# Joined 512-column high pass in channel-major products; output gates, gate logits and branch products with tokens stationary and 512 weight columns moving

## The chip, the cores and the metric

The kernel runs on one core of one Trainium2 chip. The metric is device time in microseconds, smaller is better. The matrix engine (TensorE, PE in the rows) multiplies a stationary block of 128 by 128, loaded into it first, with a moving block of up to 512 columns, and writes sums to PSUM. VectorE (DVE), ScalarE (ACT) and GpSimd (POOL) do the elementwise work; SyncE (SP) issues nearly all weight transfers.

## The reference

One layer of a decoder trunk, 256 tokens, width 2048, all in float32. Cut to what matters here:

```python
proj = jnp.einsum('bsd,de->bse', x, w_in)            # 2048 -> 14 thousand columns
(lru_x, lru_y, gla_q, gla_k, gla_v, gla_alr, gla_r,
 dn_qkv, dn_b, dn_a, dn_z, gate_logits) = jnp.split(proj, ...)
y_lru = _rg_lru_branch(lru_x, lru_y, ...)            # ends in  h * gelu(lru_y)
y_gla = _gla_branch(..., gla_r, ...)                 # ends in  rmsnorm(o) * silu(gla_r)
y_dn  = _gated_deltanet_branch(dn_qkv, ..., dn_z)    # ends in  rmsnorm(o) * silu(dn_z)
gates = jax.nn.sigmoid(gate_logits.reshape(bsz, seq, 3, D_MODEL) + b_gate)
merged = (gates[:, :, 0] * (y_lru @ w_branch[0])
          + gates[:, :, 1] * (y_gla @ w_branch[1])
          + gates[:, :, 2] * (y_dn @ w_branch[2]))
x = _layernorm(ALPHA * x + merged @ w_out, ln1_g, ln1_b)
h = jnp.square(jax.nn.relu(x @ mlp_w1 + mlp_b1)) @ mlp_w2 + mlp_b2
x = _layernorm(ALPHA * x + h, ln2_g, ln2_b)
```

## The kernel before

**Three products for one.** Each float32 operand is split into a high part in the rounded matmul type and a low part, the rest: `split` lets ACT make `hi` (line 94) and DVE make `lo` (line 95). A product is then high weight by high input, high by low, and low by high, three matmuls into one sum.

**Jobs.** All large products are a list of jobs, and `run_jobs` goes through it. A job loads 1 MB of weights (512 KB for a branch product), splits them, multiplies, and evacuates. The loads and splits of the next job stand ahead of the products of this one; `raw`, `hi` and `lo` have three buffers each, and a job uses one `raw` and two of `hi` and `lo`.

**Two layouts.** A channel-major job (`jobB`, `mmB`, lines 121 to 140) holds one 128x128 weight tile stationary, and the 256 tokens move: the sum `accB` has 128 channels by 256 tokens. It has 16 tiles of the contraction, so 48 matmuls of 256 columns; the weight tile `hi` is loaded once for `xh` (124) and once for `xl` (125). A token-major job (GLA's values, `accV`, lines 467 to 469; the output product `accO`; the second MLP product `accM`) holds 128 tokens stationary and moves 512 weight columns: 24 matmuls of 512 columns per job.

**The order of the work.** Four channel tiles together with x itself (`acc0`), then the projections of RG-LRU, GLA and DeltaNet, then for each of the three branches b sixteen pairs of one gate job (`evac_gate`) and one branch job (`job_branch`, `evac_branch`: 24 matmuls), with the eight jobs of DeltaNet's output gate behind b = 0. Then the output product, the norm, the first MLP product (`js`, 64 channel tiles, of which three go with the norm, `accH`), and the second.

**Mixers.** The small steps of the recurrences (`gen_small`, `gen_lru`, `gen_gla`, `gen_dn_*`) are generators that `pump` advances between the jobs, by a budget of DVE and ACT time per job. The Tile framework then orders the instructions of each engine and sets the semaphores; each engine runs its own queue in order.

Of the kernel before, what the change touches and what calls it, by code (L numbers as in the profile page):

```python
# [25 lines left out]
# columns of the packed per-channel parameters  # L26
# [8 lines left out]
C_BG = C_DN_G + 1  # L35
C_B1 = C_BG + 48
# [6 lines left out]
# columns of the packed constants  # L43
# [10 lines left out]
# columns of the parameters that are needed later  # L54
# [4 lines left out]
# rows of the small projections in their channel tile  # L59
# [6 lines left out]
def trunk_kernel(ctx, tc, xw, xtok, par, lat, con, wab, wa2, wB, wV, wBr, wO, w1, w2a, w2b, rows, out):  # L66
# [23 lines left out]
    def t1_tile(name, shape, dt=F32):  # L90
        return sm.tile(shape, dt, tag="t1", name=name, bufs=6)
# [6 lines left out]
    xh = [big.tile([P, 8, T], F32R, tag="xh", name=f"xh{i}", bufs=2) for i in range(2)]  # L98
    xl = [big.tile([P, 8, T], F32R, tag="xl", name=f"xl{i}", bufs=2) for i in range(2)]
# [21 lines left out]
    def mmB(acc, job, rh, rl, part, start, stop):  # L121
# [7 lines left out]
    def jobB(src, evac, rh=None, rl=None):  # L129
        rh, rl = rh or xh, rl or xl  # L130
        job = Job(src, 8 * len(rh), None, None)

        def mm():
            acc = mm_tile("accB")
            n = len(rh)
            for i in range(n):
                mmB(acc[:, :T], job, rh[i], rl[i], i, i == 0, i == n - 1)
            evac(acc[:, :T])
# [24 lines left out]
    # ---- inputs that the first jobs need  # L163
    # x and the first four channel tiles together, one slice of the contraction at a time
# [11 lines left out]
    for k in range(KT):  # L176
# [10 lines left out]
        for i in range(G0):  # L187
            o = acc0[i][:, :T]
            te.matmul(o, lhsT=h[:, i, :], rhs=kh, start=k == 0, stop=False)
            te.matmul(o, lhsT=h[:, i, :], rhs=kl, start=False, stop=False)  # L190
            te.matmul(o, lhsT=l[:, i, :], rhs=kh, start=False, stop=k == KT - 1)
# [25 lines left out]
    def col(c):  # L217
        return pt[:, c:c + 1]
# [9 lines left out]
    bgh = const.tile([P, 48], F32, name="bgh")  # L228
    ve.tensor_scalar(bgh, pt[:, C_BG:C_BG + 48], 0.5, None, ALU.mult)
# [3 lines left out]
    # ---- small projections: GLA's low rank, beta and decay of DeltaNet  # L233
# [9 lines left out]
    def evac_small(acc):  # L243
        ve.tensor_scalar(zs, acc, col(C_DTB), col(C_SGN), ALU.add, ALU.mult)
        live.append(gen_small())

    def gen_small():
        # GLA's log decay: 16 gk per head
# [47 lines left out]
        # beta, g: token rows  # L296
# [19 lines left out]
        # GLA: cumulated log decay in chunks of 64, and its exponentials  # L316
# [15 lines left out]

    yh = {}
# [6 lines left out]
    # ---- LRU  # L340
# [10 lines left out]
    def evac_lru_x(k):  # L351
        def f(acc):
            if k % 4 == 0:
                lru["xc", k // 4] = b4_tile("xc", [P, 4, T])
            conv(acc, lru["xc", k // 4][:, k % 4, :], C_LRU_W + 4 * k, col(C_LRU_B + k))
        return f

    def evac_lru_y(k):
        def f(acc):
            if k % 4 == 0:  # L360
                lru["y", k // 4] = b4_tile("yb", [P, 4, T])
            sc.copy(lru["y", k // 4][:, k % 4, :], acc)
# [4 lines left out]
    def gen_lru(hf):  # L367
# [14 lines left out]
        # gelu  # L382
# [32 lines left out]
    # ---- GLA  # L415
    gla = {}

    def evac_gla_q(h):
        def f(acc):
            if h == 0:  # L420
                gla["qe"] = b4_tile("qe", [P, 4, T])
            ve.scalar_tensor_tensor(gla["qe"][:, h, :], acc, P ** -0.5, gla["eb"][:, h, :], ALU.mult, ALU.mult)
        return f

    def evac_gla_k(h):
        def f(acc):
            if h == 0:
                gla["ke"] = b4_tile("ke", [P, 4, T])
                gla["kd"] = b4_tile("kd", [P, 4, T])
            ve.tensor_tensor(gla["ke"][:, h, :], acc, gla["enb"][:, h, :], ALU.mult)  # L430
# [3 lines left out]
    def silu2(acc, dst, use_act=True):  # L434
        """dst = 2 silu(acc)"""
# [4 lines left out]
    def evac_gla_r(k):  # L440
        def f(acc):
            if k % 4 == 0:
                gla["r", k // 4] = b4_tile("rr", [P, 4, T])
            silu2(acc, gla["r", k // 4][:, k % 4, :])
            if k == 7:
                live.append(gen_gla())
        return f

    def jobs_gla_v():
        gla["v"] = {}  # L450
        accs = {}
        jobs = []
        for nh in range(2):
            for kg in range(4):
                job = Job(wV[nh, kg], 16, None, None)

                def mm(job=job, nh=nh, kg=kg):
                    if kg == 0:
                        accs[nh] = [mm_tile("accV") for _ in range(NT)]
                    for k4 in range(4):  # L460
                        k = 4 * kg + k4
                        hi = job.hi[k4 // 2].rearrange("p k c -> p (k c)")[:, (k4 % 2) * 512:(k4 % 2) * 512 + 512]
                        lo = job.lo[k4 // 2].rearrange("p k c -> p (k c)")[:, (k4 % 2) * 512:(k4 % 2) * 512 + 512]
                        for tt in range(NT):
                            sh = xh[k // 8][:, k % 8, tt * P:(tt + 1) * P]
# [878 lines left out]
```

## Time and profile before

| | |
|---|---|
| median of 3 runs | 1744.58 us (1744.1 to 1745.21) |
| span of the profiled execution, first to last instruction | 1743.0 us |
| PE busy | 1722.7 us (99%), 12782 matmuls |
| DVE, ACT, POOL busy | 61%, 51%, 4% |
| bytes moved | 319.96 MB, mean 184 GB/s |

The time of the profiled execution itself is its span of 1743.0 us and about 1.6 us around it, if it ran as the median run did. A matmul's printed duration runs to the modelled end of its pipeline and overlaps the next one; how fast PE goes is read from the distance between two starts.

### The profile page before, as it was taken

How to read it: one execution, taken by the hardware profiler on the slowest of the kernel's cores; microseconds unless marked ns; L12 is line 12 of the kernel's file. 1: busy time of each engine (PE TensorE's matmuls, PEld its weight loads, DVE VectorE, ACT ScalarE, POOL GpSimd, SP SyncE). 2: the span in 40 equal slices, each digit the busy share in tenths (PEclk: the TensorE clock that was granted, in tenths of full speed). 3: DMA queues.
4: the chain of work that ended last, by engine and by line, in shares of the span. 5: the costliest groups of instructions: out<-in, count | busy, mean ns of one | idle time of the engine just before them, and what ended most of it. 6: DMA issues, size and time to landing. Idle time of an engine off the chain costs nothing.

```text
span 1743.0 us, 30261 instructions
## 1 busy us (share of the span) xinstructions
PE 1722.7 (99%) x12782; PEld 1644.9 (94%) x12782; DVE 1058.2 (61%) x1353; ACT 889.8 (51%) x1209; POOL 76.7 (4%) x112
## 2 busy tenths in 40 slices
PE   8999999999999999999999999999999999999997
PEld 8999898999999999999998899999999988888897
DVE  7876456876765585565555675444444455576767
ACT  6785445785344443444444455554545444455553
POOL 0000000000120203000000000000000000000000
PEclk9999999999999999999999999999999999999999
DMA  8445543444564446355566835555545455555552
GB/s 328 150 170 187 197 173 125 166 170 149 184 194 148 161 170 187 130 181 182 184 217 223 308 109 209 190 177 187 187 177 193 172 192 195 194 193 193 203 193 97
DMA packets 52536, 319.96 MB, mean 184 GB/s; under 512 B 6752, under 2 KB 7136, under 8 KB 18992
## 3 DMA queue, kind: packets, MB, share of 16 engines
q1 hardware_dynamic: 49280, 310.92, 50.3%
q0 software_dynamic: 2976, 6.84, 1.5%
q8 instruction: 100, 1.64, 0.4%
q14 instruction: 36, 0.29, 0.0%
q10 hardware_dynamic: 144, 0.26, 0.0%
HBM read 315.09 MB, written 2.88 MB: 182 GB/s over the span
## 4 chain that ended last, share of the span: by engine, by line
PE 97%; DVE 1%; DMA 1%; ACT 0%; issue 0%; SPq 0%; DVEq 0%
PE accB L124 19%; PE accB L127 19%; PE accB L125 19%; PE accM L1200 7%; PE accM L1201 7%; PE accM L1199 7%; PE accB L982 3%; PE accB L984 3%; PE accB L986 3%; PE accO L917 1%; PE accO L915 1%; PE accO L916 1%; PE accV L467 1%; PE accV L469 1%; PE accV L468 1%; DMA raw<-in_w_dram 0%
## 5 line engine op out<-in xcount | busy, mean ns | idle before, releaser
L95 DVE TENSOR_TENSOR lo<-raw,hi 128x1024 fp32r<-128x1024 f32 (+2 forms) x584 | 708.6, 1216 | 541.6 <-ACT hi L94 537.8
L94 ACT CAST hi<-raw 128x1024 fp32r<-128x1024 f32 (+2 forms) x584 | 602.4, 1034 | 757.1 <-PE accB L125 406.0
L124 PE MATMUL accB<-xh,hi 128*128 128x256 f32 x1744 | 431.0, 285 | 0.0
L125 PE MATMUL accB<-xl,hi 128*128 128x256 f32 x1744 | 427.9, 283 | 0.0
L124 PEld LDWEIGHTS accB<-xh,hi 128*128 128x128 f32 x1744 | 334.4, 192 | 2.4 <-issue 1.4
L125 PEld LDWEIGHTS accB<-xl,hi 128*128 128x128 f32 x1744 | 334.5, 192 | 0.4
L127 PE MATMUL accB<-xh,lo 128*128 128x256 f32 x1744 | 244.9, 283 | 0.0
L124 PE MATMUL accB<-x1h,hi 128*128 128x256 f32 x976 | 239.7, 283 | 0.0
L125 PE MATMUL accB<-x1l,hi 128*128 128x256 f32 x976 | 239.5, 283 | 0.0
L127 PEld LDWEIGHTS accB<-xh,lo 128*128 128x128 f32 x1744 | 225.0, 192 | 0.1
L1200 PE MATMUL accM<-hi,hl 128*128 128x512 f32 (+1 forms) x608 | 212.8, 350 | 0.0
L1199 PE MATMUL accM<-hi,hh 128*128 128x512 f32 (+1 forms) x608 | 212.8, 350 | 0.0
L1201 PE MATMUL accM<-lo,hh 128*128 128x512 f32 (+1 forms) x608 | 212.8, 350 | 0.0
L125 PEld LDWEIGHTS accB<-x1l,hi 128*128 128x128 f32 x976 | 187.4, 192 | 0.0
L124 PEld LDWEIGHTS accB<-x1h,hi 128*128 128x128 f32 x976 | 187.4, 192 | 0.0
L127 PE MATMUL accB<-x1h,lo 128*128 128x256 f32 x976 | 137.0, 283 | 0.0
L1199 PEld LDWEIGHTS accM<-hi,hh 128*128 128x128 f32 x608 | 115.1, 189 | 15.1
L1200 PEld LDWEIGHTS accM<-hi,hl 128*128 128x128 f32 x608 | 115.1, 189 | 15.0
L1201 PEld LDWEIGHTS accM<-lo,hh 128*128 128x128 f32 x608 | 115.1, 189 | 14.8
L127 PEld LDWEIGHTS accB<-x1h,lo 128*128 128x128 f32 x976 | 125.9, 192 | 0.0
L982 PE MATMUL accB<-yh,hi 128*128 128x256 f32 x384 | 109.8, 286 | 0.0
L986 PE MATMUL accB<-yh,lo 128*128 128x256 f32 x384 | 108.7, 283 | 0.0
(308 smaller groups left out, 1861.3 us busy)
## 6 DMA issues: line engine op xcount, KB each, us to landing
raw<-in_wB_dram SPq DMA_DIRECT2D x109, 1024.0 KB, 4.8
raw<-in_w_dram SPq DMA_DIRECT2D x64, 1024.0 KB, 4.8
raw<-in_w2a_dram SPq DMA_DIRECT2D x32, 1024.0 KB, 4.8
raw<-in_w2b_dram SPq DMA_DIRECT2D x32, 1024.0 KB, 4.8
raw<-in_wBr_dram SPq DMA_DIRECT2D x48, 512.0 KB, 3.4
raw<-in_wO_dram SPq DMA_DIRECT2D x16, 1024.0 KB, 4.9
raw<-in_wV_dram SPq DMA_DIRECT2D x8, 1024.0 KB, 4.8
raw<-in_xw_dram SPq DMA_DIRECT2D x15, 384.0 KB, 8.0
```

Source lines behind the costliest of these rows:

```text
L94: i1 = sc.copy(hi, raw)
L95: i2 = ve.tensor_tensor(lo, raw, hi.bitcast(F32), ALU.subtract)
L124: te.matmul(acc, lhsT=hi[:, k, :], rhs=rh[:, k, :], start=start and k == 0, stop=False)
L125: te.matmul(acc, lhsT=hi[:, k, :], rhs=rl[:, k, :], start=False, stop=False)
L127: te.matmul(acc, lhsT=lo[:, k, :], rhs=rh[:, k, :], start=False, stop=stop and k == 7)
L467: te.matmul(accs[nh][tt], lhsT=sh, rhs=hi, start=k == 0, stop=False)
L982: te.matmul(acc[:, :T], lhsT=job.hi[0][:, 4 * i + k, :], rhs=yh[b][i][:, k, :], start=i == 0 and k == 0, stop=False)
L984: te.matmul(acc[:, :T], lhsT=job.hi[0][:, 4 * i + k, :], rhs=yl[b][i][:, k, :], start=False, stop=False)
L986: te.matmul(acc[:, :T], lhsT=job.lo[0][:, 4 * i + k, :], rhs=yh[b][i][:, k, :], start=False, stop=i == 1 and k == 3)
L1199: te.matmul(t, lhsT=sh, rhs=hi, start=k == 0, stop=False)
L1200: te.matmul(t, lhsT=sl, rhs=hi, start=False, stop=False)
L1201: te.matmul(t, lhsT=sh, rhs=lo, start=False, stop=k == NK2 - 1)
```

## The change

Three things are changed, and the mathematics is the same.

Channel-major jobs hold the high and the low part of the input side by side (`pairs`, tiles `xx` of 2 x 256 tokens). One matmul of 512 columns takes the place of the two of 256 with the same weight tile; the left half of the sum is high by high, the right half high by low. The low weights go by the 256 high columns into the left half. `both` adds the halves: ACT copies the right one, DVE adds the left. `evac_h` has this add too, and its square moves from ACT to DVE.

GLA's output gate r, DeltaNet's output gate z, the gate logits and the branch products become token-major jobs (`jobs_tok`), with 4 blocks of 512 columns per 2048. All of them load 1 MB per job now. The gate's bias was a per-channel operand of ACT; it is now a row that POOL's queue loads into one buffer for each block (`load_bg`), and DVE adds it.

The merged sum is then token-major, so it is transposed on PE ahead of the output product (`gen_merged`: 4 blocks x 2 x 4 = 32 transposes of 128x128). Both branch gates are now multiplied in ahead of the transposes that these branches had already, and the split behind them reads PSUM directly (`to_branch_scaled`).

```diff
+    def pairs(name):
+        t = [big.tile([P, 8, 2, T], F32R, tag="xx", name=f"{name}{i}", bufs=2) for i in range(2)]
+        return t, [v[:, :, 0, :] for v in t], [v[:, :, 1, :] for v in t]
...
         for k in range(8):
-            te.matmul(acc, lhsT=hi[:, k, :], rhs=rh[:, k, :], start=start and k == 0, stop=False)
-            te.matmul(acc, lhsT=hi[:, k, :], rhs=rl[:, k, :], start=False, stop=False)
+            te.matmul(acc, lhsT=hi[:, k, :], rhs=flat(r[:, k]), start=start and k == 0, stop=False)
         for k in range(8):
-            te.matmul(acc, lhsT=lo[:, k, :], rhs=rh[:, k, :], start=False, stop=stop and k == 7)
...
+            te.matmul(acc[:, :T], lhsT=lo[:, k, :], rhs=r[:, k, 0, :], start=False, stop=stop and k == 7)
+
+    def both(acc, dst=None):
+        s = dst if dst is not None else t1_tile("sum", [P, T])
+        sc.copy(s, acc[:, T:])
+        ve.tensor_tensor(s, acc[:, :T], s, ALU.add)
+        return s
...
-            conv(acc, c, C_DN_W + 4 * k)
+            conv(both(acc), c, C_DN_W + 4 * k)
...
+    def jobs_tok(src, nkg, rows_of, evac, nm):
+        accs = []
+        jobs = []
+        for kg in range(nkg):
+            job = Job(src[kg], 16, None, None)
+            def mm(job=job, kg=kg):
+                if kg == 0:
+                    accs.extend(mm_tile(nm) for _ in range(NT))
+                for k4 in range(4):
+                    k = 4 * kg + k4
...
+                    rh, rl = rows_of(k)
+                    for tt in range(NT):
+                        sh, sl = rh[:, tt * P:(tt + 1) * P], rl[:, tt * P:(tt + 1) * P]
+                        te.matmul(accs[tt], lhsT=sh, rhs=hi, start=k == 0, stop=False)
+                        te.matmul(accs[tt], lhsT=sl, rhs=hi, start=False, stop=False)
+                        te.matmul(accs[tt], lhsT=sh, rhs=lo, start=False, stop=k == 4 * nkg - 1)
+                if kg == nkg - 1:
+                    for tt in range(NT):
+                        evac(tt, accs[tt])
...
-            sc.activation(t, acc, AF.Tanh, scale=0.5, bias=bgh[:, b * 16 + d:b * 16 + d + 1])
+    def load_bg(b, cb):
+        t = sm.tile([P, 512], F32, tag="bg", name="bgrow", bufs=1)
+        gp.dma_start(t, bg[b:b + 1, cb * 512:(cb + 1) * 512].to_broadcast([P, 512]))
+        gates["row"] = t
...
+            ve.tensor_tensor(t, acc, gates["row"], ALU.add)
+            sc.activation(t, t, AF.Tanh, scale=0.5)
...
-            ve.scalar_tensor_tensor(u, t, 1.0, acc, ALU.add, ALU.mult)
-            gp.tensor_tensor(m, m, u, ALU.add)
...
+            ve.scalar_tensor_tensor(t, t, 1.0, acc, ALU.add, ALU.mult)
+            gp.tensor_tensor(m, m, t, ALU.add)
+            if b == 2 and tt == NT - 1:
+                live.append(gen_merged(cb))
...
+        for kp in range(2):
+            p = mx_tile("p_m")
+            for a in range(2):
+                c = (cb % 2) * 512 + (2 * kp + a) * P
+                for tt in range(NT):
+                    te.transpose(p[:, a * T + tt * P:a * T + (tt + 1) * P], mg[tt, cb // 2][:, c:c + P], ident)
...
     for b in range(3):
-        for d in range(16):
-            jobs.append(jobB(wB[65 + b * 16 + d], evac_gate(b, d)))
-            jobs.append(job_branch(b, d))
+        for cb in range(4):
+            hooks[len(jobs)] = lambda b=b, cb=cb: load_bg(b, cb)
+            jobs += jobs_tok(wG[b, cb], 4, x_rows, evac_gate(b, cb), "accG")
+            if (b, cb) == (2, 0):
+                hooks[len(jobs)] = finish
+            jobs += jobs_tok(wBr[b, cb], 2, y_rows(b), evac_branch(b, cb), "accY")
...
-            sc.activation(t, acc, AF.Relu, bias=col(C_B1 + c))
-            sc.activation(h[c // 4][:, c % 4, :], t, AF.Square)
+            sc.activation(t, acc[:, T:], AF.Identity, bias=col(C_B1 + c))
+            ve.tensor_tensor(t, acc[:, :T], t, ALU.add)
+            ve.scalar_tensor_tensor(h[c // 4][:, c % 4, :], t, 0.0, t, ALU.max, ALU.mult)
```

How the instructions stand now is shown at three places. First PE, at the end of the second channel-major job, where GLA's first small product `p_gk` comes in. Before:

```order
L125 MATMUL accB<-xl_78,hi 128x256
L127 MATMUL accB<-xh_76,lo 128x256 x8
L258 MATMUL p_gk<-zs,wa_sb 128x256 x4
L124 MATMUL accB<-xh_75,hi 128x256
L125 MATMUL accB<-xl_77,hi 128x256
```

In the changed kernel (`xx_75` and `xx_76` are the two halves of the joined input):

```order
L131 MATMUL accB<-xx_76,hi 128x512 x8
L133 MATMUL accB<-xx_76,lo 128x256 x8
L267 MATMUL p_gk<-zs,wa_sb 128x256 x4
L131 MATMUL accB<-xx_75,hi 128x512 x8
L133 MATMUL accB<-xx_75,lo 128x256 x8
```

Sixteen alternating matmuls of 256 columns became eight of 512; the low pass and the place of the mixer's product stayed.

Second DVE, in the first stage, between the two splits `lo` of the third job. Before:

```order
L95 TENSOR_TENSOR lo_534<-raw_531,hi_533 128x1024
L349 SCALAR_TENSOR_TENSOR xc_432<-accB_474,pt_116,xc_432 128x255
L269 COPY lw_608<-lt_409 128x8
L272 SCALAR_TENSOR_TENSOR le_605<-lz_604 128x256
L349 SCALAR_TENSOR_TENSOR xc_432<-accB_474,pt_116,xc_432 128x254
L95 TENSOR_TENSOR lo_538<-raw_531,hi_537 128x1024
```

In the changed kernel:

```order
L94 TENSOR_TENSOR lo_463<-raw_460,hi_462 128x1024
L362 SCALAR_TENSOR_TENSOR xc_367<-sum_382,pt_114,xc_367 128x254
L139 TENSOR_TENSOR sum_449<-accB_416,sum_449 128x256
L362 SCALAR_TENSOR_TENSOR xc_367<-sum_382,pt_114,xc_367 128x253
L94 TENSOR_TENSOR lo_467<-raw_460,hi_466 128x1024
```

The add of the halves (`sum_449`) stands between the splits, and the convolution of the first four tiles (`sum_382`) has slid to here, one job later than before.

Third POOL's queue, around DeltaNet's first triangular inverse (`md` to `dDT` are its round trips through memory). Before:

```order
L694 MEMSET X 32x1024
L695 MEMSET X 32x32
L710 DMA xd<-X 8x32x32 x4
L710 DMA xtd<-mb 8x32x32 x4
L715 MEMSET dD 128x1024
L715 MEMSET dDT 128x1024
L718 DMA dD<-xd 32x8x32 x4
L718 DMA dDT<-xtd 32x8x32 x4
```

In the changed kernel (`bgrow` is the one buffer of the gate's bias):

```order
L710 MEMSET X 32x1024
L881 DMA bgrow<-in_bg_dram 128x512
L711 MEMSET X 32x32
L731 MEMSET dD 128x1024
L731 MEMSET dDT 128x1024
L881 DMA bgrow<-in_bg_dram 128x512
L726 DMA xd<-X 8x32x32 x4
L726 DMA xtd<-mb 8x32x32 x4
L734 DMA dD<-xd 32x8x32 x4
L734 DMA dDT<-xtd 32x8x32 x4
L881 DMA bgrow<-in_bg_dram 128x512 x2
```

Each load of the row waits until DVE has read the row before, and stands in one queue with the inverse's transfers, ahead of some and behind others.

## Rows read from the trace of the kernel before

**Rows 1.** Page: span, and busy time of each engine.

```profile
span 1743.0 us, 30261 instructions
PE 1722.7 (99%) x12782; PEld 1644.9 (94%) x12782; DVE 1058.2 (61%) x1353; ACT 889.8 (51%) x1209; POOL 76.7 (4%) x112
```

**Rows 2.** Page: chain that ended last, shares of the span by engine.

```profile
PE 97%; DVE 1%; DMA 1%; ACT 0%; issue 0%; SPq 0%; DVEq 0%
```

**Rows 3.** Waits of PE, all of them: for whom, total us, times, longest.

```profile
PE acc L189 <- ACT hi L94: 4.2, 2, 3.8
PE p_x L1077 <- DVE xt L1069: 2.0, 1, 2.0
PE accO L917 <- DVE lo L95: 1.3, 1, 1.3
PE acc L191 <- DVE lo L95: 0.2, 1, 0.2
```

**Rows 4.** Timeline of PE in a channel-major job: start, duration, instruction.

```profile
301.53 0.28 PE L124 MATMUL accB<-xh,hi 128*128 128x256 f32 x1
...
302.97 0.28 PE L124 MATMUL accB<-xh,hi 128*128 128x256 f32 x1
```

**Rows 5.** Timeline of PE in a token-major job.

```profile
179.69 0.39 PE L468 MATMUL accV<-hi,xl 128*128 128x512 f32 x1
...
185.81 0.39 PE L468 MATMUL accV<-hi,xl 128*128 128x512 f32 x1
```

**Rows 6.** Timeline of PE around four transposes.

```profile
744.65 0.28 PE L986 MATMUL accB<-yh,lo 128*128 128x256 f32 x1
744.77 0.60 PE L848 MATMUL p_dot<-ct,do 128*128 128x128 f32 x4
...
745.32 0.28 PE L125 MATMUL accB<-xl,hi 128*128 128x256 f32 x1
```

**Rows 7.** Windows by stage: length, busy us (instructions) by engine, clock, DMA share, GB/s.

```profile
29.80:160.40 130.60, 130.60 (x1056) 129.10 (x1055) 100.48 (x133) 96.31 (x130) 0.00 (x0) 1.00 0.49 177
...
249.80:403.70 153.90, 153.90 (x1231) 145.93 (x1230) 118.16 (x195) 102.45 (x163) 0.00 (x0) 1.00 0.44 154
403.70:910.60 506.90, 506.90 (x4231) 503.98 (x4231) 307.14 (x440) 216.61 (x296) 67.01 (x91) 1.00 0.52 173
...
1025.90:1377.00 351.10, 351.10 (x2929) 351.10 (x2928) 163.79 (x137) 179.84 (x252) 1.62 (x3) 1.00 0.52 185
```

**Rows 8.** Groups of DVE by shape: count | busy, mean ns | idle before.

```profile
L95 DVE TENSOR_TENSOR lo<-raw,hi 128x1024 fp32r<-128x1024 f32 x565 | 696.3, 1234 | 539.0 <-ACT hi L94 535.6 <-ACT th L437 1.9 <-PE accB L127 0.8
...
L349 DVE SCALAR_TENSOR_TENSOR cv<-accB,pt,cv 128x254 f32<-128x254 f32 x24 | 11.5, 479 | 0.4
...
L878 DVE SCALAR_TENSOR_TENSOR mg<-gate,accB 128x256 f32<-128x256 f32 x16 | 6.6, 415 | 17.2 <-PE accB L986 17.2
...
L1170 DVE TENSOR_TENSOR xt<-accM,xt 128x512 f32<-128x512 f32 x6 | 4.0, 684 | 0.7 <-PE accM L1201 0.7
```

**Rows 9.** Groups of ACT by shape.

```profile
L1038 ACT ACTIVATE h<-hr 128x256 f32<-128x256 f32 x64 | 26.7, 418 | 1.9
...
L362 ACT COPY yb<-accB 128x256 f32<-128x256 f32 x8 | 2.9, 364 | 0.0
```

**Rows 10.** Windows of 25 us, columns as in rows 7.

```profile
25.00:50.00 25.00, 25.00 (x201) 24.35 (x200) 22.14 (x44) 16.87 (x26) 0.00 (x0) 1.00 0.66 247
...
325.00:350.00 25.00, 25.00 (x207) 24.80 (x206) 22.46 (x37) 18.58 (x30) 0.00 (x0) 1.00 0.49 171
```

**Rows 11.** Timelines of DVE and PE: one split, and the pass that reads it.

```profile
58.24 1.22 DVE L95 TENSOR_TENSOR lo<-raw,hi 128x1024 fp32r<-128x1024 f32 x1
...
62.83 1.12 PE L127 MATMUL accB<-xh,lo 128*128 128x256 f32 x8
```

**Rows 12.** Groups of POOL by shape.

```profile
L882 POOL TENSOR_TENSOR mg<-mg,gb 128x256 f32<-128x256 f32 x32 | 26.0, 813 | 262.1 <-DVE gb L881 262.1
```

**Rows 13.** DMA issues: count, KB each, median us to landing.

```profile
r_g<-in_rows_dram POOLq DMA_DIRECT2D x4, 512.0 KB, 7.0
```

More of the change, by code (lines that the diff above doesn't have):

```diff
@@ L90, in t1_tile @@
     def t1_tile(name, shape, dt=F32):
-        return sm.tile(shape, dt, tag="t1", name=name, bufs=6)
+        return sm.tile(shape, dt, tag="t1", name=name, bufs=7)
     def split(raw, hi, lo):
@@ L96, in split @@
         return i1, i2
-    xh = [big.tile([P, 8, T], F32R, tag="xh", name=f"xh{i}", bufs=2) for i in range(2)]
-    xl = [big.tile([P, 8, T], F32R, tag="xl", name=f"xl{i}", bufs=2) for i in range(2)]
+    def pairs(name):
+        t = [big.tile([P, 8, 2, T], F32R, tag="xx", name=f"{name}{i}", bufs=2) for i in range(2)]
+        return t, [v[:, :, 0, :] for v in t], [v[:, :, 1, :] for v in t]
+    xx, xh, xl = pairs("xx")
     class Job:
@@ L361, in f @@
                 lru["y", k // 4] = b4_tile("yb", [P, 4, T])
-            sc.copy(lru["y", k // 4][:, k % 4, :], acc)
+            both(acc, lru["y", k // 4][:, k % 4, :])
             if k % 4 == 3:
@@ new lines, in x_rows, with evac_gla_v, f, evac_silu @@
+    def x_rows(k):
+        return xh[k // 8][:, k % 8, :], xl[k // 8][:, k % 8, :]
+    def evac_gla_v(nh):
+        def f(tt, acc):
+            if nh == 0:
+                gla["v", tt] = b4_tile(f"v{tt}", [P, 4, 256])
+            (sc.copy if tt else ve.tensor_copy)(
+                gla["v", tt].rearrange("p h c -> p (h c)")[:, nh * 512:(nh + 1) * 512], acc)
+        return f
+    def evac_silu(dic, nm, nh, after=None):
+        def f(tt, acc):
+            if nh == 0:
+                dic[nm, tt] = b4_tile(nm, [P, 1024])
+            t = t2_tile("th", [P, 512])
+            sc.activation(t, acc, AF.Tanh, scale=0.5)
+            ve.scalar_tensor_tensor(dic[nm, tt][:, nh * 512:(nh + 1) * 512], t, 1.0, acc, ALU.add, ALU.mult)
+            if nh == 1 and tt == NT - 1 and after:
+                live.append(after())
+        return f
@@ L996, in trunk_kernel @@
         if b == 0:
-            for k in range(8):
-                jobs.append(jobB(wB[57 + k], evac_dn_z(k)))
+            for nh in range(2):
+                jobs += jobs_tok(wZ[nh], 4, x_rows, evac_silu(dn, "dz", nh), "accZ")
     n_mix = len(jobs)
@@ L1017, in before_out @@
     def before_out():
[L1018 removed]
         dummy = sm.tile([P, 1], F32, tag="dummy", name="dummy", bufs=1)
[L1020 removed]
+        sc.activation(dummy, gates["row"][:, 0:1], AF.Sqrt, scale=0.0, bias=eps[:, 3:4])
         for tt in range(NT):
@@ L1025, in before_out @@
                 nc.sync.dma_start(xt[tt, i], xtok[tt * P:(tt + 1) * P, i * 1024:(i + 1) * 1024])
-    x1h = [big.tile([P, 8, T], F32R, tag="xh", name=f"x1h{i}", bufs=2) for i in range(2)]
-    x1l = [big.tile([P, 8, T], F32R, tag="xl", name=f"x1l{i}", bufs=2) for i in range(2)]
+    xx1, x1h, x1l = pairs("xx1")
     h = []
@@ L1268, in lay_out @@
     small[:, R_A:R_A + 8] = da
-    wB = np.concatenate([tiles(t) for t in (small, lx, ly, gq, gk, gr, qkv, dz, gl)], 0)
-    wBr = np.stack([tiles(f["w_branch"][b]) for b in range(3)], 0)
+    wB = np.concatenate([tiles(t) for t in (small, lx, ly, gq, gk, qkv)], 0)
+    wG = np.stack([blocks(gl[:, b * D:(b + 1) * D], 4, 512) for b in range(3)], 0)
+    wBr = np.stack([blocks(f["w_branch"][b], 4, 512) for b in range(3)], 0)
     def ch(v):
```

212 lines of the change are left out of this document (83 added, 129 removed).

## The prediction

> **What bounds the kernel now.** I began with the page. PE is busy for 1722.7 of 1743.0 us [rows 1], and the chain that ended last lies on PE for 97% of the span [rows 2]. A busy PE may still wait inside its pipeline, so the view of PE's waits comes next: the reader is to see that it has four lines, 7.7 us in all, at the start and around the first norm [rows 3]. So for nearly all of the span PE issues without a pause, and what counts is the distance between its starts. It is read in two stretches without mixers. In a channel-major job 12 steps take 302.97 - 301.53 = 1.44 us, 120.0 ns for 256 columns [rows 4]. In a token-major job 27 steps take 185.81 - 179.69 = 6.12 us, 226.7 ns for 512 columns [rows 5]. Two matmuls of 256 cost 240.0 ns and one of 512 costs 226.7: **13.3 ns for each pair that becomes one**. The granted clock is 1.00 in all four stages of rows 7, the upper level of 2.4 GHz, so no change of clock is in this difference.
>
> The windows by stage then say how far the other engines are from taking over: DVE has 100.5 of 130.6 us in the first projections, 118.2 of 153.9 in DeltaNet's, 307.1 of 506.9 in gates and branches, 163.8 of 351.1 in the first MLP product [rows 7]. PE does not wait for it anywhere there [rows 3], but finer windows reach 22.1 and 22.5 of 25 [rows 10].
>
> **The change, part by part.** *Pairs joined.* Channel-major: the first four tiles 4 x 16 = 64 pairs, 45 jobs of 16 that keep this layout 720, the first MLP product 61 x 16 = 976 and its three tiles that go with the norm 48. Token-major: r and z lose 16 x 48 matmuls of 256 and get 16 x 24 of 512, so 384 pairs; the gate logits 48 x 24 = 1152; the branch products 48 x 12 = 576. Together 3920. The 48 beside the norm I count at nothing, since PE waits there for DVE already [rows 3]; if they did count it would be 0.6 us. 3872 x 13.33 ns = **-51.6 us**.
>
> For the branch, gate, r and z products the price is that of a row of the same form: tokens stationary, 512 weight columns moving [rows 5]. For the channel-major join no row shows 512 columns against a stationary weight tile. I take the same 226.7, because both are a 128x128 load and 512 float32 columns; the other bound is 240, where 1808 of the pairs give nothing (24.1 us less).
>
> The Trainium skill's page TensorE: Matmul & The Clock Gate, section Back-to-back issue gap, speaks against a gain of this size: it gives the gap of a lone stream as columns over 2.4 GHz plus about 2.5 ns, so 109 ns for 256 columns and 216 for 512, and a pair that is joined would save only that 2.5 ns. By that, 3872 pairs give 9.7 us. This case's rows have 120.0 and 226.7, so each start costs 13.3 ns beyond its columns here, and they decide.
>
> *Transposes of the merged sum.* 32 more on PE. Four of them moved the matmuls behind by 0.43 us: the second matmul after them starts at 745.32, and at the steady 120 ns it would have been 744.65 + 2 x 0.12 = 744.89 [rows 6]. So 0.108 us each, **+3.5 us**. They wait for POOL's add. Behind the last product of a block DVE needs 0.68 us per token half [rows 8], and POOL two adds of 512 columns, each some 1.6 us as twice its 0.81 for 256 [rows 12] (an estimate): some 4 us. They stand 24 matmuls, 5.4 us, behind that product, so I count no wait; if DVE has two splits of 1.23 us [rows 8] ahead of the evacuation it is about 1 us for each of the four blocks.
>
> *The adds of the halves.* Each of 45 jobs and 4 first tiles gets an ACT copy (0.364 us [rows 9]) and a DVE add (0.42, as the 256-column DVE reading PSUM [rows 8]). An MLP job gets two DVE instructions of 0.42 and loses ACT's square of 0.418 [rows 9]. Nothing of this is on PE; what hides it is PE's own time, and what is late if the cover goes is the split `lo`, for which PE waits. By stage:
> First projections, 21 jobs and the four tiles: DVE 100.5 + 25 x 0.42 = 111.0; PE 130.6 - 21 x 0.213 = 126.1, so 88%. In the hottest window DVE goes from 22.1 to some 25.5 (4 tiles, 4 jobs) against 24.1 us of PE: over by 1.4. The cover is the lead: a split that ends at 58.24 + 1.22 = 59.46 is read at 62.83, 3.4 us later [rows 11]. From 28 us to there DVE gets 9 adds, 3.8 us, and PE comes 1.1 us earlier, so this lead is used up. ACT also carries two table loads more. I take **2 us** of waits, bounds 0 and 5.
> DeltaNet's projections, 24 jobs: 118.2 + 10.1 - 3 (GLA's tail loses eight 0.42 us instructions) = 125 of 148.8, 84%; the hottest window 22.5 + 1.8 = 24.3 of 24.1. **1 us**, bounds 0 and 4.
> Gates and branches: 24 bias adds of 0.68 and smaller items give DVE about 12 us more: 319 of 485, 66%. But the triangular inverses and the chain of small products behind them share DVE with evacuations that are now 0.68 long. **1 us**, bounds 0 and 3.
> First MLP product: DVE 163.8 + 61 x 0.84 = 215 of 338, 64%; ACT falls to 154. Nothing; a job has 2 us of DVE to spare, and without that cover each 0.1 us per job would cost 6.
> Together **+4 us** (0 to 12).
>
> *The bias row.* 12 loads of 256 KB on POOL's queue, one buffer. The row is read a whole block (four jobs, 21.8 us) after it is asked for; 512 KB from the same queue land in 7.0 us [rows 13]. Nothing.
> *Transfers.* Gates and branches needed 1.5 MB in 48 x 120 + 24 x 120 ns = 8.64 us, now 1 MB in 5.44: 193 GB/s on demand, as the first MLP stage draws 185 [rows 7]. Nothing; the weight queue waits for nothing new.
>
> **The sum.** -51.6 + 3.5 + 4 = -44.1 us against the profiled span of 1743.0: 1698.9. The median of the runs is 1.6 us above the span, 1744.58, so **1700.5 us**.
>
> **The rivals.**
> *DVE comes too late.* The waits are 10 to 25 us rather than 4, since order within a queue and not mean load decides. For it: hottest windows over 100%. Against it: before, windows at 90% made PE wait not once [rows 3, 10]. 1706 to 1722 us.
> *The weight-stationary join gives little.* If what a matmul costs beyond its columns stayed with the halves, 1808 pairs would give nothing: 1724.6; if no pair of either layout gave more than about 2.5 ns, 1742.4. Against it: rows 5 have the same columns at 226.7 ns. The second of these is where the page's formula would put it.
> *More than the sum.* No waits, and the 48 pairs count: 1695.9, or a little less with the waits at the norm shortened.
> *Slower, by the bias row.* DVE's add of a block waits for the row, the splits queue behind the add, and PE behind the splits. In POOL's queue the row stands behind the inverse's transfers, or behind the last reader of its one buffer. A row that misses its block by x makes PE wait about x - 3.4 (the lead of rows 11). It is slower only when that adds to more than 48 us, 4 us in each of 12 blocks, so if rows land some 29 us after the asking; 7.0 us speaks against it. From 1748 us.
> *It does nothing:* the 3920 issues were hidden behind something else. PE's unbroken pace speaks against it. 1744.6.
>
> **How the numbers follow.** Forecast (1695.5 to 1706) 0.73; late DVE 0.13; join of little worth 0.05; more than the sum 0.04; slower 0.03; nothing 0.02. The range of eight in ten is the forecast, down to 1694 for the case above it and up to 1712 for the near half of late DVE: about 0.82. A measurement of this kernel tells about 0.2% from no change, 3.5 us; faster has 0.95, same 0.02, slower 0.03.
>
> **What would show each step.** The distance of starts in the eight joined matmuls should be 226.7 ns, and a channel-major job 8 x 2 x (226.7 + 120) = 5.55 us instead of 5.76. From the first gate to the output product it should be about 484 us instead of 506.9, the first MLP product 338 instead of 351.1. PE's waits should name `lo` on DVE before 130 us and around 300 to 400, a few us in all. The transposes should show no wait for POOL over 1 us. I am wrong if the joined distance is near 240, or if waits for DVE pass 12 us; a wait of DVE for the bias row would show the slower rival.

## The result and the profile after

The changed kernel takes 1711.41 us (median of 4 runs, 1710.71 to 1714.08) where the kernel before takes 1744.34: 0.9816 of its time, 95% interval 0.9802 to 0.983. It is clear of no change and faster, as forecast, but by 33 us where 44 were forecast. The profiled execution has a span of 1709.4 us, 33.6 less than before.

The page of the changed kernel, which answers to [rows 1]:

```profile
span 1709.4 us, 22528 instructions
...
PE 1683.4 (98%) x8894; PEld 1443.0 (84%) x8894; DVE 1126.4 (66%) x1511; ACT 877.7 (51%) x1164; POOL 85.8 (5%) x108
```

There are 3888 fewer matmuls, as counted (3920 joined, 32 transposes more). PE's waits, all of them, beside [rows 3]:

```profile
PE acc L201 <- ACT hi L93: 6.8, 2, 4.2
PE p_bg L312 <- DVE lr L308: 2.6, 1, 2.6
PE p_x L1103 <- DVE xt L1095: 1.3, 1, 1.3
PE p_x L1103 <- issue: 1.1, 1, 1.1
PE p_i L753 <- DVE q L746: 1.0, 1, 1.0
PE accB L133 <- DVE lo L94: 0.4, 1, 0.4
PE accB L131 <- ACT hi L93: 0.3, 1, 0.3
```

The first line is at the very start, where before it was 4.2 us in two waits; the waits on `p_bg`, `accB` and `p_i` are new, and that on `accO` is gone. Where the rest went is read from the time between the first matmuls of the stages, in both traces:

| from the first matmul of ... to that of ... | before | after | difference | forecast |
|---|---|---|---|---|
| start of the span to the first job | 29.79 | 33.93 | +4.1 | -0.9 |
| first job to GLA's values | 130.61 | 131.70 | +1.1 | -2.5 |
| GLA's values to the first gate (values, r, DeltaNet) | 250.58 | 243.90 | -6.7 | -6.7 |
| first gate to the output product | 499.66 | 479.09 | -20.6 | -22.0 |
| output product to the transposes of the norm | 90.01 | 90.45 | +0.4 | +0.9 |
| these to the second MLP product | 376.33 | 364.58 | -11.8 | -13.0 |
| second MLP product to the end | 366.02 | 365.75 | -0.3 | 0 |

The last column puts the forecast's terms where they belong: the pairs of each stage at 13.3 ns, 24 transposes in the gates' stage and 8 in the output product's, the waits of 2, 1 and 1 us. (The cut at 403.70 in rows 7 lies 7.3 us early, a good job: before, the first gate job starts at 410.98. That moved these 7.3 us between two stages of the forecast, and left its sum as it was.) Most of the gap of 10.5 us is in the first two lines, before any of the new token-major jobs has run. The windows of the two long stages, columns as in rows 7:

```profile
33.93:165.63 131.70, 128.25 (x720) 111.24 (x719) 107.59 (x158) 104.13 (x148) 0.00 (x0) 1.00 0.48 167
...
409.53:888.62 479.09, 478.11 (x2274) 398.21 (x2273) 312.75 (x435) 211.21 (x272) 72.80 (x85) 1.00 0.55 190
```

In the first projections PE loses 3.4 of 131.7 us while DVE is busy for 82% and ACT for 79%. Mean load names no culprit.

**The distance of the joined matmuls.** Timeline of PE in a gate job and in a job of the first MLP product:

```profile
412.05 0.39 PE L474 MATMUL accG<-lo,xx 128*128 128x512 f32 x1
...
414.77 0.39 PE L474 MATMUL accG<-lo,xx 128*128 128x512 f32 x1
...
1100.63 2.00 PE L131 MATMUL accB<-xx,hi 128*128 128x512 f32 x8
1102.47 1.12 PE L133 MATMUL accB<-xx,lo 128*128 128x256 f32 x8
...
1106.22 2.00 PE L131 MATMUL accB<-xx,hi 128*128 128x512 f32 x8
```

In the gate job 12 steps take 2.72 us, 226.7 ns each, the price that was taken. In the channel-major job eight joined matmuls take 1.84 us, 230 ns each in the mean, and a whole job 1106.22 - 1100.63 = 5.59 us (5.587 over 50 jobs) where 5.547 were forecast. That is 5.76 - 5.587 = 0.173 us for 16 pairs, 10.8 ns a pair and not 13.3. The starts one by one say where the rest is (means over 114 half jobs of this stage): the first five joined matmuls behind a low pass are 228 to 236 ns apart, the last three 226.7, and the first low one takes 113.3, the others 119 to 120. So the price that was taken is reached within the eight, and what is lost stands at the change of form.

**The start.** Timeline of ACT: the conversion of x's second slice in the kernel before.

```profile
6.16 0.41 ACT L94 CAST xh<-raw 128x256 fp32r<-128x256 f32 x1 [1.97 <-DMA raw<-in_xw_dram]
```

In the changed kernel, ACT's conversions of the first two slices and PE around its wait:

```profile
3.20 0.40 ACT L93 CAST xx<-raw 128x256 fp32r<-128x256 f32 x1 [1.18 <-DMA raw<-in_xw_dram]
...
6.70 0.41 PE L202 MATMUL acc<-xx,lo 128*128 128x256 f32 x1
...
8.74 0.40 ACT L93 CAST xx<-raw 128x256 fp32r<-128x256 f32 x1 [4.52 <-DMA raw<-in_xw_dram]
...
9.75 0.77 PE L201 MATMUL acc<-xx,hi 128*128 128x512 f32 x1 [2.64 <-ACT hi L93]
...
14.66 0.63 PE L201 MATMUL acc<-xx,hi 128*128 128x512 f32 x1
...
15.30 0.63 PE L201 MATMUL acc<-xx,hi 128*128 128x512 f32 x1
...
15.91 0.39 PE L201 MATMUL acc<-xx,hi 128*128 128x512 f32 x1
...
16.26 0.40 PE L201 MATMUL acc<-xx,hi 128*128 128x512 f32 x1
```

The view of the bias row's tile, its loads (duration of the issue, start of the first and of the last):

```profile
L881 POOL DMA_DIRECT2D bgrow<-in_bg_dram x12: 543/564/709, 1.4 to 845.5; - x12
```

Before, the second slice was converted at 6.16 us. Now that comes at 8.74, and the first load of the bias row has gone out at 1.4 us: POOL's queue is empty then, and the buffer is free. PE stands for 2.6 us, and afterwards runs at half pace for another 6 us: 0.64 us from one joined matmul to the next, 768 columns with the low one between them, which is the pace of the lower level of 1.2 GHz (the clock column does not show it, see the last section), until 15.7, then 0.35, the upper level. Before, the full pace began at 7.87 us. That the row's load delays the slice, and the slice PE, is so far read from the order of events; row_late tests it.

**The waits at 60 to 68 us.** Timeline of ACT in the kernel before, the last two of its loads here:

```profile
49.77 1.28 ACT L283 ACT_TABLE_LOAD   x1
...
53.08 1.28 ACT L285 ACT_TABLE_LOAD   x1
```

In the changed kernel, ahead of the waits, with one row of DVE and one of PE:

```profile
51.33 1.28 ACT L292 ACT_TABLE_LOAD   x1
...
53.06 1.28 ACT L294 ACT_TABLE_LOAD   x1
...
55.73 1.28 ACT L292 ACT_TABLE_LOAD   x1
...
57.14 0.35 ACT L138 COPY yb<-accB 128x256 f32<-128x256 f32 x1
57.51 1.28 ACT L294 ACT_TABLE_LOAD   x1
57.53 0.42 DVE L139 TENSOR_TENSOR yb<-accB,yb 128x256 f32<-128x256 f32 x1 [3.15 <-ACT yb L138]
...
59.03 1.28 ACT L292 ACT_TABLE_LOAD   x1
...
62.34 1.28 ACT L294 ACT_TABLE_LOAD   x1
...
68.00 0.44 PE L312 MATMUL p_bg<-ct,lr 128*128 128x128 f32 x2 [2.56 <-DVE lr L308]
```

A table load is an instruction that ACT runs here ahead of a change between Ln and Exp. Ln (line 292) and Exp (294) of three inputs now come in three rounds, six table loads of 1.28 us in 12 us; before (lines 283 and 285) there were two rounds and four loads, the first two at 40.70 and 43.74 us. The waits view names DVE, but DVE stands idle for 3.15 us here, for the copy of a half that ACT does late.

### The profile page after: what moved, and what is told of

Same layout as the page of the kernel before. It is cut to its first block, busy times and chain, and to the rows that moved or that the text cites. A ratio compares the mean times of both kernels' runs of the same rounds, so it can differ in the third digit from the quotient of the medians.

```text
span 1709.4 us, 22528 instructions
## 1 busy us (share of the span) xinstructions
PE 1683.4 (98%) x8894; PEld 1443.0 (84%) x8894; DVE 1126.4 (66%) x1511; ACT 877.7 (51%) x1164; POOL 85.8 (5%) x108
## 4 chain that ended last, share of the span: by engine, by line
PE 97%; DVE 1%; ACT 1%; DMA 0%; issue 0%; SPq 0%; DVEq 0%; ACTq 0%
PE accB L131 22%; PE accB L133 12%; PE accM L1225 7%; PE accM L1224 7%; PE accM L1223 7%; PE accG L473 5%; PE accG L474 5%; PE accG L472 5%; PE accY L473 3%; PE accY L474 3%; PE accY L472 3%; PE accO L951 2%; PE accO L949 2%; PE accO L950 2%; PE acc L201 1%; PE accZ L474 1%
## 5 line engine op out<-in xcount | busy, mean ns | idle before, releaser
L131 PE MATMUL accB<-xx,hi 128*128 128x512 f32 x1696 | 426.7, 393 | 0.3 <-ACT hi L93 0.3
L131 PEld LDWEIGHTS accB<-xx,hi 128*128 128x128 f32 x1696 | 305.4, 189 | 57.4 <-issue 1.4
L133 PEld LDWEIGHTS accB<-xx,lo 128*128 128x128 f32 x1696 | 231.1, 190 | 18.1 <-DVE lo L94 1.8
L133 PE MATMUL accB<-xx,lo 128*128 128x256 f32 x1696 | 236.8, 282 | 0.5 <-DVE lo L94 0.4
L472 PE MATMUL accG<-hi,xx 128*128 128x512 f32 x384 | 150.9, 393 | 0.0
L473 PE MATMUL accG<-hi,xx 128*128 128x512 f32 x384 | 149.9, 390 | 0.0
L474 PE MATMUL accG<-lo,xx 128*128 128x512 f32 x384 | 149.7, 390 | 0.0
L473 PEld LDWEIGHTS accG<-hi,xx 128*128 128x128 f32 x384 | 72.1, 188 | 14.6
L472 PEld LDWEIGHTS accG<-hi,xx 128*128 128x128 f32 x384 | 72.1, 188 | 14.4
L472 PE MATMUL accY<-hi,yh 128*128 128x512 f32 x192 | 74.9, 390 | 0.0
L473 PE MATMUL accY<-hi,yl 128*128 128x512 f32 x192 | 74.7, 389 | 0.0
L474 PE MATMUL accY<-lo,yh 128*128 128x512 f32 x192 | 74.7, 389 | 0.0
```

Source lines behind the costliest of these rows:

```text
L131: te.matmul(acc, lhsT=hi[:, k, :], rhs=flat(r[:, k]), start=start and k == 0, stop=False)
L133: te.matmul(acc[:, :T], lhsT=lo[:, k, :], rhs=r[:, k, 0, :], start=False, stop=stop and k == 7)
L472: te.matmul(accs[tt], lhsT=sh, rhs=hi, start=k == 0, stop=False)
L473: te.matmul(accs[tt], lhsT=sl, rhs=hi, start=False, stop=False)
L474: te.matmul(accs[tt], lhsT=sh, rhs=lo, start=False, stop=k == 4 * nkg - 1)
```

## The experiments

Each row gives the median, the ratio to the kernel before in the same session with its 95% interval, and the span of the profiled execution. The kernel before took 1744.34 us in the first session, 1745.27 in that of row_late to tok_only, 1742.49 in that of late_ln to add_twice and 1743.94 in the last, so medians of different sessions compare to some 3 us only; smaller differences between them are read from the stages of the traces, one execution of each kernel.

| run | us | ratio | span |
|---|---|---|---|
| changed kernel | 1711.41 | 0.9816 (0.9802 to 0.983) | 1709.4 |
| row_late | 1708.7 | 0.9784 (0.9766 to 0.9802) | 1704.6 |
| one_ln | 1706.58 | 0.9773 (0.9756 to 0.979) | 1704.9 |
| hi16_lo16 | 1707.21 | 0.978 (0.976 to 0.9801) | 1704.7 |
| tok_only | 1726.6 | 0.9892 (0.9875 to 0.991) | 1724.8 |
| late_ln | 1702.22 | 0.9769 (0.9752 to 0.9785) | 1700.1 |
| all_three | 1703.6 | 0.9775 (0.9761 to 0.979) | 1703.3 |
| row_wide | 1709.63 | 0.981 (0.9795 to 0.9825) | 1707.2 |
| add_twice | 1705.93 | 0.9786 (0.9772 to 0.9801) | 1703.5 |
| mlp16 | 1701.6 | 0.9756 (0.9742 to 0.9771) | 1700.3 |
| warm | 1701.77 | 0.9755 (0.9742 to 0.9768) | 1700.9 |

**row_late.** The first load of the bias row waits for a value of about 80 us.

```diff
         t = sm.tile([P, 512], F32, tag="bg", name="bgrow", bufs=1)
+        if (b, cb) == (0, 0):
+            gp.tensor_copy(t[:, 0:8], negc1)
         gp.dma_start(t, bg[b:b + 1, ...].to_broadcast([P, 512]))
```

> The first load of the bias row, which in the changed kernel has nothing to wait for and goes out in the first microseconds, is held back until about 80 us (its buffer is first written from a value of DeltaNet's decays). Theory (the 256 KB of the row take the place of x's second slice in the transfers, and PE, left idle, starts at the lower clock): x's second slice is converted near 6.2 us instead of 8.74, PE is at the full pace by about 8 us instead of 15.9, the first job of the list starts near 29.3 us instead of 33.9, and the time falls by 4 to 5 us, to about 1707. Rival (the slice came late in these runs for another reason, such as the memory or the order of x's own loads): the start stays at 33.9 us and the time within 1 us of 1711.

Timeline of ACT in this run, the conversion of the second slice:

```profile
7.03 0.40 ACT L93 CAST xx<-raw 128x256 fp32r<-128x256 f32 x1 [2.58 <-DMA raw<-in_xw_dram]
```

View of the transfers, GB/s of the first 16 us in 40 slices of 0.4 us, of this run:

```profile
GB/s 0 0 0 0 81 223 338 365 85 192 346 307 384 338 376 292 338 323 353 392 384 353 361 361 422 399 415 422 415 399 407 422 399 376 438 407 392 399 407 399
```

The same of the changed kernel:

```profile
GB/s 0 0 0 0 84 227 350 356 38 74 56 97 159 248 264 320 259 274 346 399 415 407 407 415 399 430 415 407 422 392 438 399 384 399 430 392 384 415 407 384
```

With the row on its way the transfers fall to 38 to 97 GB/s from 3.2 to 4.8 us; without it they are at 85 and 192 for 0.8 us and then back at 346. PE is at the full pace from 8.73 us, the first job starts at 29.42 instead of 33.93, and the stages behind are unchanged within 0.4 us (131.73 us for the first projections, with the same waits). Of the 4.5 us some 1.8 are the shorter stop of PE (its two starts around it are 1.26 us apart instead of 3.05), the rest the earlier rise of the clock. The rival falls. The median fell by 2.7 us only; the span of the profiled execution by 4.8. That execution was the fastest of the four, the others took 2.3 to 2.5 us more. Over all runs the two cases stay apart: with the one row read early (the changed kernel, one_ln, hi16_lo16, tok_only) the second slice is converted at 8.74 to 9.83 us and the first job starts at 33.66 to 34.89; with the row held back (this run, late_ln, all_three, add_twice, mlp16, warm) it is 6.05 to 7.03 and 29.13 to 31.45. So the early row is shown to cost time at the start; how much varies from execution to execution, 4.5 us between these two.

**one_ln.** All Exp behind all Ln.

```diff
-        for z, e, u, r in sets:
-            sc.activation(u, u, AF.Ln)
-        for z, e, u, r in sets:
-            sc.activation(r, u, AF.Exp, scale=-1.0)
+        lns = [sc.activation(u, u, AF.Ln) for z, e, u, r in sets]
+        with tc.issue_after(lns[0].ins), tc.issue_after(lns[1].ins), tc.issue_after(lns[2].ins):
+            for z, e, u, r in sets:
+                sc.activation(r, u, AF.Exp, scale=-1.0)
```

> The three Exp of GLA's and RG-LRU's decays are put behind all three Ln on ACT, so that two table loads do instead of six. Theory (ACT is late between 51 and 66 us, because four more table loads of 1.28 us stand in its queue beside the new copies of the halves): PE's waits at 60 to 68 us (0.4 for the split, 0.35 for the high part, 2.6 for the transposes of the decays) fall below 0.5 in all, time about 1708. Rival (DVE is late there, by its adds of the halves): the waits stay within 1 us of 3.4, time 1711. Second rival (the delay of the first four tiles at the start is carried into this place): waits as before, and they would go in the run with the late row instead.

PE's waits in this run, all of them:

```profile
PE acc L201 <- ACT hi L93: 7.7, 2, 4.3
PE p_x L1103 <- DVE xt L1095: 1.3, 1, 1.3
PE p_x L1103 <- issue: 1.1, 1, 1.1
PE p_i L753 <- DVE q L746: 1.0, 1, 1.0
```

Its window of the first projections, columns as in rows 7:

```profile
33.66:160.91 127.25, 127.25 (x720) 111.35 (x719) 107.52 (x158) 98.95 (x144) 0.00 (x0) 1.00 0.49 173
```

The three waits of this stage are gone and it takes 127.25 us, 4.45 less. DVE does the same work (107.5 us of 158 instructions, against 107.6), ACT has four table loads less (98.95 against 104.13): the cause was ACT's order, not DVE's adds alone. The late start is still there (33.66), so the lost lead did not cause these waits either. tok_only agrees: without the copies and adds of the halves it has two rounds and four loads as before, and its first projections take 130.61 us, as before, behind the latest start of all.

The Trainium skill's page ScalarE: Activation LUTs, section Table sets: the hidden batching unit, says to batch activations by table set, and there the trace agrees: each of the six changes was a load of 1.28 us, and four of them went when all Ln stood ahead of all Exp. It also lists Ln followed by Exp as one load, because one set holds both; here every change between the two was a load of its own.

**tok_only.** Only the token-major half.

```diff
-            te.matmul(acc, lhsT=hi[:, k, :], rhs=flat(r[:, k]), ...)
+            te.matmul(acc[:, :T], lhsT=hi[:, k, :], rhs=r[:, k, 0, :], ...)
+            te.matmul(acc[:, :T], lhsT=hi[:, k, :], rhs=r[:, k, 1, :], ...)
...
```

The first four tiles, the three tiles beside the norm and the evacuation in the first MLP product go back in the same way.

> Only the token-major half of the change: the output gates, gate logits and branch products as in the changed kernel, the channel-major products with two matmuls of 256 columns as before, without the adds of the halves. Prices by trace: 2112 pairs at 13.3 ns give 28.2 us, 32 transposes cost 3.5, and the early load of the bias row, which is still there, costs 4.4 at the start: about 1724. If the delay at the start belongs to the joined products instead, 1719.6. If a token-major pair is worth less than 13.3 ns (10.8 as in the channel-major jobs), 1729.

It took 1726.6 us. Its first job starts at 34.89 us, 5.1 later than before, with no joined product in the kernel and the bias row in it. Without those 5.1 us its span is 1743.0 - (1724.8 - 5.1) = 23.3 us below that of before, against 28.2 - 3.5 = 24.7 by the prices: with the 1.0 us that PE waits for `p_i` in this run too, 0.4 us remain. The whole alone would not decide, since it holds other differences: the stretch from the norm to the second MLP product takes 374.21 us here where it took 376.33, with nothing joined in it. The price is shown by the stretch from GLA's values to the first gate, where only the 192 pairs of r are new: 248.00 us instead of 250.58, 13.4 ns a pair. The value of 1729, for 10.8 ns in these jobs as well, is excluded by this and by the 226.7 ns of the gate job above.

**hi16_lo16.** 16 joined matmuls, then 16 low ones.

```diff
+        for part in range(2):
+            for k in range(8):
+                te.matmul(acc, lhsT=job.hi[part][:, k, :], rhs=flat(r[part][:, k]), start=part == 0 and k == 0,
+                          stop=False)
+        for part in range(2):
+            for k in range(8):
+                te.matmul(acc[:, :T], lhsT=job.lo[part][:, k, :], rhs=r[part][:, k, 0, :], start=False,
+                          stop=part == 1 and k == 7)
...
-            for i in range(n):
-                mmB(acc, job, r[i], i, i == 0, i == n - 1)
+            mmB(acc, job, r)
```

> In a channel-major job all 16 joined matmuls stand ahead of all 16 low ones, so that PE changes between the two forms twice in a job instead of four times. Theory (the 40 ns by which a job is longer than 16 x 226.7 + 16 x 120.0 come with each change from low to joined): about 20 ns per job come back, 106 jobs give 2.1 us, time about 1709.3, and a steady job of the first MLP product takes 5.567 us instead of 5.587. Rival (each joined matmul against a stationary weight tile costs 230.0 ns): a job stays at 5.587 us and the time at 1711.4.

Timeline of PE in the first MLP product:

```profile
1105.14 3.82 PE L130 MATMUL accB<-xx,hi 128*128 128x512 f32 x16
1108.79 2.08 PE L134 MATMUL accB<-xx,lo 128*128 128x256 f32 x16
1110.70 1.55 PE L130 MATMUL accB<-xx,hi 128*128 128x512 f32 x6
```

A job takes 5.56 us, 5.567 over 49 jobs: 20 ns back, as expected from two changes of form fewer. So the 40 ns belong to the changes, not to each joined matmul. The time of the whole run says less, because ACT's table loads had fallen into one round here by themselves: the first projections take 128.13 us, 3.6 less than in the changed kernel.

**late_ln, all_three.** `row_late` and `one_ln` together, and with them the order of hi16_lo16.

> Both mends together: the first bias row held back, and one round of Ln and Exp. If the delay at the start (33.93 to 29.42 us for the first job) and ACT's table loads (131.7 to 127.3 us for the first projections) are two causes, the gains add: span about 1709.4 - 4.8 - 4.5 = 1700, time about 1702. If the lead that is lost at the start is one cause of the waits at 60 to 68 us, they overlap and the time stays at 1705 to 1706.

> Both mends, and the 16 joined matmuls of a job ahead of its 16 low ones. In the run with that order alone a steady job took 5.567 us instead of 5.587, but ACT's table loads had fallen into another order there too. If 20 ns per job is all that the order gives, 106 jobs make it 2.1 us less than the run with both mends: span about 1698, time about 1700. If the low part of the first half, which is now read later, gives nothing more, the waits of PE before 160 us stay at none; a wait for the high part of the second half, which is read earlier now, would speak against it.

In the traces the two mends add: first job at 29.13 us, first projections 127.24, span 1709.4 - 9.3 = 1700.1, time 1702.22. The ratios are of different sessions and say less: 0.9784 and 0.9773 with one mend each, 0.9769 with both. The third takes nothing off: all_three has 1703.6 and a span of 1703.3. Its first MLP product is shorter (358.1 against 359.2 us from `accH`'s first matmul), but the new order moved the mixers' steps and splits elsewhere, and PE's waits show four behind the start that late_ln does not have, 3.2 us together:

```profile
PE accO L953 <- DVE lo L94: 1.5, 1, 1.5
...
PE accB L134 <- DVE lo L94: 0.9, 1, 0.9
PE p_bg L312 <- DVE lr L308: 0.5, 1, 0.5
PE accO L951 <- ACT hi L93: 0.3, 1, 0.3
```

**row_wide.** The early load reads 128 rows of memory with the same values.

```diff
-        gp.dma_start(t, bg[b:b + 1, cb * 512:(cb + 1) * 512].to_broadcast([P, 512]))
+        gp.dma_start(t, bg[b, cb])
```

> As the changed kernel, with the early load of the bias left where it is, but its 256 KB are read from 128 rows of memory that hold the same values, not 128 times from one row of 2 KB. Theory (what holds x's second slice up is the repeated reading of one row): that slice is converted near 7 us, the first job starts below 31 us and the time is 1707 to 1708. Rival (any 256 KB that another queue moves in these microseconds do it): converted after 8.5 us, first job near 33.9 us, time 1711.

The same line of the transfers' view:

```profile
GB/s 0 0 0 0 92 234 342 334 127 118 210 315 320 379 379 371 323 392 384 422 407 369 323 376 384 384 446 392 399 415 407 415 415 392 407 369 346 392 415 415
```

The hole is 127 and 118 GB/s for 0.8 us, nearly that of row_late, instead of 38 to 97 for 1.6. The second slice is converted at 7.25 us, the first job starts at 31.75, between row_late and the changed kernel; the time of 1709.63 is not clear of 1711. The theory's first job below 31 us did not come, nor the rival's slice after 8.5. In these executions reading one row 128 times is the larger part of the delay of the slice. Why the full pace then began only at 12.9 us, after a stop of 1.56 us between two starts, stays open.

**add_twice.** One more DVE instruction behind each add of `both`, on top of late_ln.

```diff
         ve.tensor_tensor(s, acc[:, :T], s, ALU.add)
+        ve.tensor_scalar(s, s, 1.0, None, ALU.mult)
```

> The run with both mends, with one more DVE instruction of 256 columns (a multiplication by 1 within SBUF, some 0.28 us) behind each add of the halves outside the MLP, 49 in all: it shows how much cover DVE still has. Theory (ACT's order was late, not DVE): the time stays within 1 us of the run with both mends. Rival (DVE is at its limit in the first projections and in DeltaNet's, as the forecast had it): half or more of 49 x 0.28 = 13.7 us appears, 7 us or more.

3.7 us more than late_ln (span 3.4), between the two, so neither holds: 13.7 us of DVE work are three quarters hidden. The largest piece is 1.4 us in the first projections (128.67 against 127.24). DVE is nearer to its limit there than the theory had it. The adds themselves fitted: with them and ACT's order mended PE is busy for all of one_ln's window.

**mlp16, warm.** late_ln with 16 and 16 in the first MLP product alone; and that with eight matmuls of zeros ahead of x.

> The run with both mends, and 16 joined matmuls ahead of 16 low ones in the first MLP product alone, so that no mixer's step can change its place. Theory (20 ns per job, and what the run with that order everywhere lost came from other places of the mixers' steps and of the output product's splits): 61 x 0.020 = 1.2 us less than the run with both mends, 1701.0, steady job 5.567 us, the stages ahead of it unchanged within 0.3 us. Rival (the order itself costs something, as a later reading of the low halves): time 1702 or more.

> As the run before this in the list, with eight matmuls of 512 zero columns on PE ahead of the first slice of x, whose result nobody reads. Theory (the lower clock at the start costs time of its own): PE is at the full pace before 6 us instead of at 9.4, the first job starts near 27 us instead of 29.1, time about 1699. Rival (the transfers of x's slices set the end of the first four tiles, whatever the clock): PE only waits longer between the slices, first job at 29 us, time 1701.

mlp16 took 1701.6 us, 0.6 less than late_ln with overlapping intervals; its job takes 5.57 us:

```profile
1100.75 3.82 PE L138 MATMUL accB<-xx,hi 128*128 128x512 f32 x16
...
1106.32 3.82 PE L138 MATMUL accB<-xx,hi 128*128 128x512 f32 x16
```

Its profiled execution came to the full pace at 13.1 us and to the first job at 31.45, so that its span hides the 1.2 us; from the first job to the end it is 1668.9 us against late_ln's 1671.0, and from `accH`'s first matmul to the second MLP product 357.93 against 359.16, the 1.2 us. In warm PE works without a stop from 1.92 to 9.3 us, and the full pace still began only at 7.8; the first job starts at 29.2, as in late_ln, and the time is 1701.77: not the 27 and 1699 of the theory. Against its own base mlp16 this execution starts the first job 2.25 us earlier and takes 2.8 us more behind it, with waits that mlp16 does not have (0.8 us on `accO`, 0.3 on `p_bg`). So no gain in time is shown; what a filled start alone does to the rise of the pace stays open. These two and late_ln are the best versions, and cannot be told apart by their times.

## Why the prediction was right and wrong

The forecast was 10.5 us too low, and the measured 1711.41 lies outside it (1695.5 to 1706). That it lies in the wide range up to 1712 is luck: the range took in the near half of "late DVE", and PE's waits named for DVE were 5.3 us here, not the 10 to 25 of that rival. Three steps failed: the bias row, put at nothing, cost 4.8 us between the profiled executions; the table loads on ACT, named without a price, 4.5; the price of the channel-major pairs, 4.4. Of the 4 us of waits that were in the sum, 1.0 came as forecast.

*What bounds, and the token-major price: right.* 226.7 ns in the new jobs, and PE loses 1.0 of 479.09 us there. The stage gained 20.6 us where the table has 22.0, with that wait in both; the 1.4 us between them were not tested.

*The channel-major price: mechanism right, size off.* "I take the same 226.7" was measured as 230.0 and 119.1 in the mean, 10.8 ns a pair; 1760 x 2.5 = 4.4 us of the sum were not there (the 24.1 us of the other bound took 1808 pairs, though the sum holds 1760 of them). A row with one form in an unbroken stream was carried over to a job that changes form four times; the other bound, 240, was not reached. That the stretch from GLA's values to the first gate met its -6.7 us is luck: its 384 channel-major pairs gave 1.0 us less, and the 1 us of waits did not come. The Trainium skill's formula for an isolated matmul (TensorE: Matmul & The Clock Gate, Back-to-back issue gap) would give, as an estimate, 215.8 and 109.2 ns and 2.5 a pair, and the traces do not bear it out.

*The transposes: right.* Around eight of them the second matmul stands at 794.57 where 793.47 + 0.23 would have been its place, 0.87 us, 0.109 each, and no wait for POOL:

```profile
793.47 1.03 PE L916 MATMUL p_m<-ct,mg 128*128 128x128 f32 x8
794.26 0.48 PE L472 MATMUL accG<-hi,xx 128*128 128x512 f32 x1
794.57 0.40 PE L473 MATMUL accG<-hi,xx 128*128 128x512 f32 x1
```

*The waits: wrong cause.* The forecast had "what is late if the cover goes is the split `lo`", by DVE's adds, 2 us in the first projections, 1 in DeltaNet's, 1 in the gates. Measured: 3.3 in the first projections by the view of waits (4.45 when undone), none in DeltaNet's, 1.0 in the gates (`p_i`). ACT's queue made the first: "ACT also carries two table loads more" was written down and given no price. The two loads more came as written, and the order that saves four gave back all 4.45 us with every add in place. The forecast's sign, a wait for `lo` on DVE before 130 us, did show, but with 0.4 us only.

*"The bias row ... Nothing": the step that failed most.* The text followed the row from the block that reads it, and asked whether a load could be late. The first one is early: it goes out at 1.4 us into the one stretch where PE hangs on the transfers, and cost 4.5 us at the start between the two profiled executions (2.7 us by the medians), through x's second slice and PE's later rise to the full pace. Where the order of POOL's queue was shown, it was shown for the middle of the program alone.

Put together: -51.6 + 4.4 (channel-major price) + 3.5 (transposes) + 4.5 (ACT's order) + 1.0 (`p_i`) + 4.8 (the early row) = -33.4 us, measured -33.6 between the spans. That it closes so well is in part luck: the 1.4 us that the gates' stage lacks stand against 1.2 us that the stretch from the norm to the second MLP product gained beyond its jobs, 11.8 - 61 x 0.173. Neither was tested; the second is not the joining's work, since tok_only gains 2.1 us there with no joined product.

## What to carry to other kernels

A transfer that has nothing to wait for goes out at the start, wherever it stands in the program: here at 1.4 us, for a reader at 436.2. When a change adds one on an idle queue, look at the first microseconds. Where an engine has to fit a few instructions more, look at the order of its whole queue, table loads first, and not at its busy share; the engine that the waits view names may itself stand idle for another. And take the price of a matmul from a row that changes its form as often as the new code does.

## What was not expected of the hardware

- A change between 512 and 256 moving columns, with stationary weights: two changes cost 20 ns beyond 226.7 and 120.0 per matmul (5.587 against 5.567 us a job with four and with two). The change of weights alone cost nothing: a job before had it too, at 256 columns throughout, and took 48 x 120.0 ns = 5.76 us.
- In one execution each, 256 KB read as 128 times one row of 2 KB held all transfers at 38 to 97 GB/s for 1.6 us; read from 128 rows at 118 to 127 for 0.8 us, little worse than without (85 and 192).
- PE's pace at the start rose late after a long stop: at 14.2 to 15.9 us in the four executions with 2.7 to 4.4 us between two starts, at 7.8 to 9.4 us in six others, but twice at 12.9 and 13.1 us with 1.56 and 0.81 us between two starts, which stays open: row_late had 1.26 and rose at 8.73. While the pace was half, the clock column of the windows (of the changed kernel) printed 1.00:

```profile
9.75:15.70 5.95, 5.95 (x17) 4.77 (x18) 4.87 (x10) 4.43 (x10) 0.00 (x0) 1.00 1.03 407
```
